# A two-layer encoder trunk on one core: order of the first norms, 20 weight subtractions behind the score's reciprocal, and one row block scaled in column halves

## The chip, the cores and the metric

The kernel runs on one core of a Trainium2 chip. The metric is the device time of one execution in microseconds (us). Before the change three runs gave 2630.57, 2634.04 and 2635.19 us; the median is 2634.04. The profile is one execution more, of 2632.38 us.

## The reference

2048 rows (frames) of 1024 numbers go through a gated MLP layer (A) and an attention layer (B), with residual adds and a last norm. All is float32.

```python
def gmlp_mixer(h, w_in, ln_g, ln_b, w_s, b_s, w_out):
    u, v, z = jnp.split(h @ w_in, 3, axis=-1)          # 1024 -> 3 x 2048
    v = layer_norm(jax.nn.gelu(v), ln_g, ln_b)
    ...
    mixed = jnp.einsum('hts,bgshc->bgthc', w_m, vg)    # within groups of 128 rows
    ...
    return (jax.nn.gelu(u) * mixed * jax.nn.silu(z)) @ w_out

def chunk_attention_mixer(h, k_pad, v_pad, w_qz, rel_bias, w_out):
    q, z = jnp.split(h @ w_qz, 2, axis=-1)
    ...
        sc = jnp.einsum('bqhd,bkhd->bhqk', qc, kc) + bias   # own chunk of 64 and 8 before
        p = jax.nn.softmax(sc, axis=-1)
        ... p @ v
    return (o * jax.nn.silu(z)) @ w_out

x = x + gmlp_mixer(rms_norm(x, a_norm_g), ...)
k, v = rms_norm(x, g_kv) @ w_kv
x = x + chunk_attention_mixer(rms_norm(x, b_norm_g), k, v, ...)
return rms_norm(x, final_norm_g)
```

## The kernel before

**Products.** A matrix product in float32 is made of three matmuls in a faster type: each operand is split into a high half (a rounded copy) and a low half (the rest), and `mm3` (lines 111 to 117) issues high x high (113) and the two mixed products (114, 115; for the projections 115 is the one with the weight's low half). A split is two instructions: ACT copies the high half, then DVE subtracts it to get the low half. For weights this is `split_in` (242 to 245): the copy is line 243, the subtraction 244. For layer A's activations and weight sums it is `split` (465 to 470, subtraction 469), for other left operands lines 362 and 367. Large products use Strassen's form with seven products, so sums of blocks are made on POOL and DVE as well.

**Start of the program (layer A, first rows).** Blocks of 128 rows are normed by `block_norm`: ACT sums the squares, DVE adds the epsilon (`power`, 744), POOL raises it to -1/2 (745), DVE scales the row (`scale`, 749). `ha0` to `ha7` are the even blocks, `hb0` on the odd ones (their `r` is `ra0` to `ra15`). PE then transposes them (643) into PSUM tiles `t0_ph_j`, and `split` makes the left operands `S0_ph_j` out of them, which frees the tile. The weight sums `T0_...`, `T1_...` are split by the same function. While `begin` is set, `first("dve", ...)` chains DVE's instructions in the order in which the code issues them.

**Attention.** Loops run over four blocks t of 512 rows, eight pairs p of heads, and eight steps u (two heads by four blocks of 128 rows). In a step `score` (1540) issues the score matmuls `s` (1555) of two steps ahead, DVE adds the bias and takes the peak in one instruction (`pr`, `nm`, 1563), ACT takes the exponential (1573), DVE the reciprocal of the sum (`sl`, 1576), POOL multiplies (1577). `flip` transposes the probabilities (`tp`, 1593), ACT copies and DVE subtracts (1597, 1598) into `pt`, and `value` multiplies by V (`pv`, 1618). Between these, PE works at the projections of the next pair: `pj{t}_{p}_{c}` with c = 1 for the queries, 0 for the keys, 2 for the gate, each of eight `mm3` on the weights `wh_b{t}_{p}_{c}` and `wl_b{t}_{p}_{c}` that `weights` (256) loads and splits, and at the output product `bo` of the block of rows before. The queries come out by ACT and DVE (`Qh`, `Ql`, 1484 and 1485), the keys by 1499 and 1500.

**Last rows.** When both halves of a block of 128 rows are done, `finish` (1908) makes its norm factor (`rr_f`), loads the row again from `x2d` and queues `scale` (1934; the DVE instruction is line 1937) in `finals`, one of which is taken in each step u and in `last_all`. Output goes through SP. In block t = 3 and pair p = 7 the rows `y2_0` to `y2_3` of block 2 are finished beside the last scores `s3_15_...`, and then `last_all` makes the output product of block 3.

**Who sets the order.** A scheduler places the instructions of all engines by its own estimates of their times; each engine then runs its list in order. Manual dependencies (`behind`, `follow`, `on_beat`, `paced`) only constrain that order, without a semaphore. SP issues most of the DMAs.

## Time and profile before

| | |
|---|---|
| time, median of three runs | 2634.04 us |
| profiled execution: time, span | 2632.38 us, 2630.6 us |
| mean granted TensorE clock | 0.998 |
| moved by DMA | 727.65 MB, 277 GB/s in the mean |
| 128 x 512 matmuls of line 113 in layer A's first products | 1248, 397 ns each as the profile counts them |
| peak (1563), exponential (1573), multiply (1577) of the scores | 256 each, 736, 764 and 814 ns in the mean |
| subtraction for attention's weights (244) | 96, 1256 ns in the mean |

Matmuls overlap in a pipeline, so a duration of 397 ns does not mean one each 397 ns: in the timeline they start some 0.23 us apart. Idle time of an engine is shown in square brackets, with what ended it.

### The profile page before, as it was taken

What the parts mean: (1) busy time and instruction counts of PE and PEld (TensorE: products, weight loads), DVE (VectorE), ACT (ScalarE), POOL (GpSimd) and SP (SyncE); (2) the same over time, 40 slices, a digit from 0 to 9 for tenths busy, and PEclk for the clock granted to TensorE, in tenths of its full rate; (3) what the DMA queues carried; (4) which work ended last, traced back from release to release, by engine and by line L of the source; (5) the groups of instructions that cost most, each with busy time, mean ns of one, the idle gap of its engine ahead of it and who ended that gap; (6) DMA issues with size and microseconds to landing.
All of it is one profiled execution on the core that took longest, in us unless ns stands there. A gap on an engine that the chain in (4) does not pass through costs nothing. (4 is left out here: it accounts for less than half of the span.)

```text
span 2630.6 us, 38030 instructions
## 1 busy us (share of the span) xinstructions
PE 2605.7 (99%) x12976; PEld 2180.0 (83%) x12976; DVE 1865.7 (71%) x2932; ACT 1311.1 (50%) x2327; POOL 891.9 (34%) x871
## 2 busy tenths in 40 slices
PE   9999999999999999999999999999999999999998
PEld 7888888888888888888888878888888888888886
DVE  6655676766667667757776767777777777876777
ACT  5422243443433434343466466666666655666554
POOL 4611335243152332302334334344333232332235
PEclk9999999999999999999999999999999999999999
DMA  7899998989988968967977587778787667875678
GB/s 290 316 345 331 344 377 311 326 317 340 329 300 306 333 225 309 344 201 261 335 267 250 170 286 234 233 240 265 251 264 264 224 207 221 289 231 185 210 231 302
DMA packets 277169, 727.65 MB, mean 277 GB/s; under 512 B 29168, under 2 KB 69104, under 8 KB 276976
## 3 DMA queue, kind: packets, MB, share of 16 engines
q1 hardware_dynamic: 268816, 707.13, 78.2%
q10 hardware_dynamic: 8160, 18.09, 1.9%
q8 instruction: 104, 1.70, 0.3%
q14 instruction: 89, 0.73, 0.1%
HBM read 535.84 MB, written 178.78 MB: 272 GB/s over the span
## 5 line engine op out<-in xcount | busy, mean ns | idle before, releaser
L113 PE MATMUL P<-T,S 128*128 128x512 f32 x1248 | 495.5, 397 | 0.0
L115 PE MATMUL P<-T,S 128*128 128x512 f32 x1248 | 488.3, 391 | 0.1
L114 PE MATMUL P<-T,S 128*128 128x512 f32 x1248 | 487.7, 391 | 0.0
L1577 POOL TENSOR_SCALAR pr<-pr,sl 128x640 f32<-128x640 f32 (+4 forms) x256 | 208.4, 814 | 551.5 <-DVE sl L1576 472.6
L113 PE MATMUL pj<-hh_b,wh_b 128*128 128x512 f32 x768 | 318.1, 414 | 0.0
L115 PE MATMUL pj<-hh_b,wl_b 128*128 128x512 f32 x768 | 304.4, 396 | 0.3 <-DVE wl_b L244 0.2
L114 PE MATMUL pj<-hl_b,wh_b 128*128 128x512 f32 x768 | 302.7, 394 | 0.0
L1573 ACT ACTIVATE pr<-pr,nm 128x640 f32<-128x640 f32 (+4 forms) x256 | 195.5, 764 | 193.8 <-DVE nm L1563 191.8
L115 PEld LDWEIGHTS P<-T,S 128*128 128x128 f32 x1248 | 234.5, 188 | 50.9 <-DVE S L469 0.4
L114 PEld LDWEIGHTS P<-T,S 128*128 128x128 f32 x1248 | 235.3, 189 | 45.1 <-DVE T L469 0.3
L113 PEld LDWEIGHTS P<-T,S 128*128 128x128 f32 x1248 | 235.1, 188 | 44.6 <-DVE vst L670 0.2
L1598 DVE TENSOR_TENSOR pt<-tp,pt 128x640 fp32r<-128x640 f32 (+4 forms) x256 | 188.8, 737 | 47.2 <-ACT pt L1597 44.2
L1563 DVE CUSTOM_DVE_ANT_0 pr<-s,bias 128x640 f32<-128x640 f32 (+4 forms) x256 | 188.3, 736 | 45.0 <-PE s L1555 38.1
L1597 ACT CAST pt<-tp 128x640 fp32r<-128x640 f32 (+4 forms) x256 | 159.0, 621 | 41.4 <-PE tp L1593 35.8
L115 PEld LDWEIGHTS pj<-hh_b,wl_b 128*128 128x128 f32 x768 | 144.2, 188 | 34.5 <-DVE wl_b L244 2.7
L1593 PE MATMUL tp<-ident,pr 128*128 128x128 f32 x1120 | 166.5, 274 | 4.7 <-DVE pt L1598 4.4
L1593 PEld LDWEIGHTS tp<-ident,pr 128*128 128x128 f32 x1120 | 130.6, 140 | 39.0 <-issue 11.9
L1618 PEld LDWEIGHTS pv<-pt,V 128*128 128x128 f32 x896 | 144.2, 190 | 19.5 <-DVE pt L1598 3.6
L113 PEld LDWEIGHTS pj<-hh_b,wh_b 128*128 128x128 f32 x768 | 145.0, 189 | 17.8 <-ACT wh_b L243 1.2
L114 PEld LDWEIGHTS pj<-hl_b,wh_b 128*128 128x128 f32 x768 | 145.0, 189 | 16.8
L1618 PE MATMUL pv<-pt,V 128*128 128x256 f32 (+3 forms) x896 | 155.8, 321 | 0.6 <-DVE pt L1598 0.5
L244 DVE TENSOR_TENSOR wl_b<-raw_b,wh_b 128x1024 fp32r<-128x1024 f32 x96 | 120.5, 1256 | 25.1 <-ACT wh_b L243 24.1
(309 smaller groups left out, 5711.7 us busy)
## 6 DMA issues: line engine op xcount, KB each, us to landing
S<-hsd SPq DMA_DIRECT2D x288, 512.0 KB, 5.5
rw<-in_w_a SPq DMA_DIRECT2D x108, 512.0 KB, 6.4
raw_b<-wk SPq DMA_DIRECT2D x75, 512.0 KB, 4.4
A<-ytd SPq DMA_DIRECT2D x72, 512.0 KB, 5.7
hsd<-S SPq DMA_DIRECT2D x56, 512.0 KB, 4.6
V<-vhd SPq DMA_DIRECT2D x56, 512.0 KB, 5.3
bias<-reld SPq DMA_DIRECT2D x64, 320.0 KB, 3.9
va<-vd SPq DMA_DIRECT2D x32, 512.0 KB, 5.5
```

The lines of the kernel that those rows point to most:

```text
L113: first = mm(ps, lh, rh, start=first, stop=False)
L114: mm(ps, lh, rl, start=False, stop=False)
L115: ends[0] = mm(ps, ll, rh, start=False, stop=last).ins.name
L244: tv(wl[:], raw[:], wh[:].bitcast(F32), op=sub)
L1563: peak = nc.vector.tensor_tensor_reduce(out=pr[:, c0:].rearrange("p (a b) -> p a b", a=nseg), in0=ps[:, :nseg, :w], in1=bias[:, c0:].rearr ...
L1573: nc.scalar.activation(pr[:, c0:], pr[:, c0:], AF.Exp, scale=-1.0, bias=nm[:], accum_out=sl[:])
L1577: nc.gpsimd.tensor_scalar(pr[:, c0:], pr[:, c0:], sl[:], 1.0, op0=ALU.mult, op1=ALU.mult)
L1593: ins = tpose(tp[:, b, :], pr[:, b * P : (b + 1) * P], ident[:])
L1597: nc.scalar.copy(oh, tp[:, b0:5, :].rearrange("p a b -> p (a b)"))
L1598: nc.vector.tensor_tensor(pt[:, 2560 + o + b0 * P : 2560 + o + 640], tp[:, b0:5, :].rearrange("p a b -> p (a b)"), oh.bitcast(F32), op=ALU ...
L1618: mm(po[:, q0 * P : q1 * P], vtl[t, p][:, i, hs], rhs, start=(i == blocks[0] and j == 0), stop=(i == 7 and j == 1),)
```

## The change

It has three parts, and no matmul is added or removed.

1. **Norming order.** `power` and `scale` are held in DVE's first order only for blocks below 8. The scale of an even block is issued one step later, and for blocks 10 and 12 (`ha5`, `ha6`) it goes behind the last scale. The weight subtractions of `T0_2` go behind the last scale, those of `T1_2` behind the last low half of a left operand. ACT's copy for `S0_1_4` goes behind the last square.
2. **Ties.** For the 20 weights in `BEHIND` the subtraction goes behind the reciprocal of the last score issued before it in the code (`recips`).
3. **Rows by halves.** The row `y2_3` is loaded as two halves; the scales of `y2_1` and `y2_3` are issued one column half at a time through `beside`: behind the peak of a score, in step u = 6 of the last pair, in `last_all`, or before the last value product.

```diff
--- before.py
+++ after.py
@@ -197,2 +197,3 @@
     beat = []
+    recips = []
 
@@ -241,7 +242,8 @@
 
-    def split_in(raw, wh, wl):
+    def split_in(raw, wh, wl, names=()):
         hi = nc.scalar.copy(wh[:], raw[:])
-        tv(wl[:], raw[:], wh[:].bitcast(F32), op=sub)
+        follow(tv(wl[:], raw[:], wh[:].bitcast(F32), op=sub), names)
         return hi
 
+    BEHIND = {1: ((2, 1), (3, 0), (4, 0), (5, 0), (7, 1), (7, 2)), 2: ((1, 0), (2, 2), (3, 2), (5, 1), (7, 1), (7, 0), (7, 2)), 3: ((1, 1), (1, 0), (4, 1), (4, 2), (5, 1), (7, 0), (7, 2))}
     kept = []
@@ -269,3 +271,3 @@
                 keep_all()
-        hi = split_in(raw, *w)
+        hi = split_in(raw, *w, recips if t and (p, c) in BEHIND[t] else ())
         if t:
@@ -464,3 +466,3 @@
 
-        def split(hi, lo, src, key=None):
+        def split(hi, lo, src, key=None, tie=None):
             ins = first("act", nc.scalar.copy(hi, src))
@@ -468,3 +470,6 @@
                 in_order(key, ins)
-            first("dve", nc.vector.tensor_tensor(lo, src, hi.bitcast(F32), op=sub))
+            low = first("dve", nc.vector.tensor_tensor(lo, src, hi.bitcast(F32), op=sub))
+            if tie:
+                behind(low, tie)
+            last["dve"] = low.ins.name
             return ins
@@ -530,3 +535,6 @@
                 out[q] = where(q)
-                ins = split(*out[q], vs[q])
+                tie = None
+                if n in (0, 1) and ph == 2:
+                    tie = last["low"] if n else last["scale"]
+                ins = split(*out[q], vs[q], tie=tie)
                 if n in (0, 1) and ph in (6, 4, 5, 7):
@@ -645,3 +653,6 @@
             t = s_tile(f"S0_{ph}_{j}")
-            split(t[:, 0], t[:, 1], pt[:], "S")
+            ins = split(t[:, 0], t[:, 1], pt[:], "S")
+            last["low"] = last["dve"]
+            if (ph, j) == (1, 4):
+                behind(ins, last["square"])
             later(1, lambda: paced(nc.sync.dma_start(
@@ -743,3 +754,5 @@
             def power():
-                first("dve", nc.vector.tensor_scalar(r[:], r[:], EPS, None, op0=add))
+                ins = nc.vector.tensor_scalar(r[:], r[:], EPS, None, op0=add)
+                if blk < 8:
+                    first("dve", ins)
                 ins = nc.gpsimd.tensor_tensor(r[:], r[:], mhalf[:], op=ALU.pow)
@@ -748,5 +761,10 @@
             def scale(c=slice(0, D)):
-                first("dve", nc.vector.scalar_tensor_tensor(
+                ins = nc.vector.scalar_tensor_tensor(
                     t[:, c], t[:, c], r[:], gab[:, c], op0=mul, op1=mul
-                ))
+                )
+                if blk < 8:
+                    first("dve", ins)
+                elif blk in (10, 12):
+                    behind(ins, last["scale"])
+                last["scale"] = ins.ins.name
 
@@ -971,3 +989,3 @@
             ts.setdefault(s, []).append(lambda: todo.pop(0)())
-            at(s + 1, lambda: todo.pop(0)())
+            at(s + 1 + (block is block_a and s >= 0), lambda: todo.pop(0)())
 
@@ -1572,2 +1590,4 @@
                 gating.pop(0)()
+            if beside:
+                beside.pop(0)(peaks[-1:])
             nc.scalar.activation(
@@ -1575,3 +1595,3 @@
             )
-            nc.vector.reciprocal(sl[:], sl[:])
+            recips[:] = [nc.vector.reciprocal(sl[:], sl[:]).ins.name]
             nc.gpsimd.tensor_scalar(
@@ -1625,2 +1645,3 @@
         gating = []
+        beside = []
         peaks = []
@@ -1846,2 +1867,4 @@
                             finals.pop(0)()
+                        while beside:
+                            beside.pop(0)()
                     if k == 1:
@@ -1922,5 +1945,6 @@
                     y = [row[b][:, c, :] for c in range(2)]
-                elif t + 2 == NT and b == 0:
+                elif t + 2 == NT and b in (0, 3):
                     on_beat(first)
-                    y = [half_tile("og", f"y{t}_{b}_{c}", 2)[:] for c in range(2)]
+                    tag, n = ("C", 4) if b else ("og", 2)
+                    y = [half_tile(tag, f"y{t}_{b}_{c}", n)[:] for c in range(2)]
                     for c in range(2):
@@ -1933,4 +1957,4 @@
 
-                def scale():
-                    for c in range(2):
+                def scale(cols=(0, 1), names=()):
+                    for c in cols:
                         cs = slice(c * 512, c * 512 + 512)
@@ -1939,2 +1963,3 @@
                         )
+                        follow(ins, names)
                         if not last:
@@ -1968,3 +1993,10 @@
                 else:
-                    finals[:0] = [scale] if t + 2 == NT else [lambda: None, scale]
+                    if t + 2 < NT:
+                        finals[:0] = [lambda: None, scale]
+                    elif closed:
+                        finals[:0] = [scale]
+                    else:
+                        finals[:0] = [lambda: beside.extend(
+                            lambda names=(), c=c: scale((c,), names) for c in range(2)
+                        )]
 
@@ -2126,2 +2158,4 @@
                         finals.pop(0)()
+                    if beside and (t + 1, p + 1, u) == (NT, NPAIR, 6):
+                        beside.pop(0)()
                     if todo:
@@ -2134,2 +2168,4 @@
                 before = t, p
+        while beside:
+            beside.pop(0)()
         value(*before, 1)
```

The first place is DVE at the start of the program. Before:

```order
L469 TENSOR_TENSOR T0_2_01_778<-rw0_2_100_545,T0_2_00_777 128x1024
L469 TENSOR_TENSOR T1_2_hl_851<-rw1_2_100_549,T1_2_hl_851 128x1024
L469 TENSOR_TENSOR T0_2_11_848<-rw0_2_101_547,T0_2_10_847 128x1024
L469 TENSOR_TENSOR T1_2_hl_851<-rw1_2_101_551,T1_2_hl_851 128x1024
L469 TENSOR_TENSOR S0_1_5_666<-t0_1_5_661,S0_1_5_666 128x512
L744 TENSOR_SCALAR ra5_558<-ra5_558 128x1
L749 SCALAR_TENSOR_TENSOR hb2_557<-hb2_557,ra5_558,gab_345 128x1024
L469 TENSOR_TENSOR S0_4_1_678<-t0_4_1_673,S0_4_1_678 128x512
L469 TENSOR_TENSOR S0_1_6_723<-t0_1_6_718,S0_1_6_723 128x512
L469 TENSOR_TENSOR S0_5_0_733<-t0_5_0_728,S0_5_0_733 128x512
```

After, from the scale of `hb2` on:

```order
L762 SCALAR_TENSOR_TENSOR hb2_557<-hb2_557,ra5_558,gab_345 128x1024
L471 TENSOR_TENSOR S0_1_5_665<-t0_1_5_660,S0_1_5_665 128x512
L471 TENSOR_TENSOR T0_2_01_778<-rw0_2_100_545,T0_2_00_777 128x1024
L471 TENSOR_TENSOR S0_4_1_677<-t0_4_1_672,S0_4_1_677 128x512
L471 TENSOR_TENSOR T0_2_11_848<-rw0_2_101_547,T0_2_10_847 128x1024
L471 TENSOR_TENSOR S0_1_6_722<-t0_1_6_717,S0_1_6_722 128x512
L471 TENSOR_TENSOR S0_5_0_733<-t0_5_0_728,S0_5_0_733 128x512
L471 TENSOR_TENSOR S0_1_7_774<-t0_1_7_769,S0_1_7_774 128x512
L471 TENSOR_TENSOR S0_5_1_789<-t0_5_1_784,S0_5_1_789 128x512
L471 TENSOR_TENSOR S0_4_2_798<-t0_4_2_793,S0_4_2_798 128x512
L471 TENSOR_TENSOR S0_2_0_844<-t0_2_0_839,S0_2_0_844 128x512
L471 TENSOR_TENSOR T1_2_hl_851<-rw1_2_100_549,T1_2_hl_851 128x1024
```

`S0_4_1` had the four weight subtractions ahead of it and now has one; the two of `T1_2_hl` stand behind `S0_2_0` and `S0_2_1`.

The second place is one tie, `wl_b3_1_0`, on DVE. Before, from that subtraction on (the reciprocal of `s3_1_0` stands two rows below the last one here):

```order
L244 TENSOR_TENSOR wl_b3_1_0_22635<-raw_b3_1_0_22633,wh_b3_1_0_22634 128x1024
L1576 RECIPROCAL sl3_0_2_22509<-sl3_0_2_22509 128x1
L367 TENSOR_TENSOR Slo2_1_1_22857<-A2_00_22514,Sho2_1_1_22856 128x512
L1640 TENSOR_TENSOR og32_2_7_22364<-pv2_15_22535,ot2_15_22561 64x512
L1598 TENSOR_TENSOR pt3_0_22552<-tp3_0_0_22553,pt3_0_22552 128x640
L1563 ISA pr3_0_3_22575,nm3_0_3_22576<-s3_0_3_22570,bias3_0_22259 128x640
L1563 ISA nm3_0_3_22576 128x1
L1648 SCALAR_TENSOR_TENSOR og2_7_22579<-og32_2_7_22364,Z2_7_22226 128x512
L1576 RECIPROCAL sl3_0_3_22577<-sl3_0_3_22577 128x1
L1598 TENSOR_TENSOR pt3_0_22552<-tp3_0_1_22592,pt3_0_22552 128x640
L1563 ISA pr3_1_0_22611,nm3_1_0_22612<-s3_1_0_22606,bias3_1_22463 128x640
L1563 ISA nm3_1_0_22612 128x1
```

After:

```order
L1581 ISA pr3_1_0_22611,nm3_1_0_22612<-s3_1_0_22606,bias3_1_22463 128x640
L1581 ISA nm3_1_0_22612 128x1
L1503 SCALAR_TENSOR_TENSOR Ql3_1_0_22622<-pj3_1_1_22531,Qh3_1_0_22621 64x512
L1961 SCALAR_TENSOR_TENSOR y1_0_22497<-y1_0_22497,rr_f1_0_22493,gf_13671 128x512
L1596 RECIPROCAL sl3_1_0_22613<-sl3_1_0_22613 128x1
L245 TENSOR_TENSOR wl_b3_1_0_22635<-raw_b3_1_0_22633,wh_b3_1_0_22634 128x1024
L1503 SCALAR_TENSOR_TENSOR Ql3_1_1_22628<-pj3_1_1_22531,Qh3_1_1_22627 64x512
L1618 TENSOR_TENSOR pt3_0_22552<-tp3_0_2_22643,pt3_0_22552 128x640
L1961 SCALAR_TENSOR_TENSOR y1_0_22497<-y1_0_22497,rr_f1_0_22493,gf_13671 128x512
```

The subtraction went from behind `Slo2_1_0` to behind the reciprocal `sl3_1_0`, and `Ql3_1_0` and the first half of `y1_0` stand ahead of that reciprocal. PE at the same place, before, from the score `s3_1_0` on:

```order
L1555 MATMUL s3_1_0_22606<-K3_0_1_22411,Qh3_0_1_22304 128x320 x2
L1555 MATMUL s3_1_0_22606<-K3_0_1_22411,Ql3_0_1_22305 128x320 x2
L113 MATMUL pj3_1_1_22531<-hh_b_13392,wh_b3_1_1_22526 128x512
L114 MATMUL pj3_1_1_22531<-hl_b_13393,wh_b3_1_1_22526 128x512
L115 MATMUL pj3_1_1_22531<-hh_b_13392,wl_b3_1_1_22527 128x512
L113 MATMUL pj3_1_0_22639<-hh_b_13392,wh_b3_1_0_22634 128x512
L114 MATMUL pj3_1_0_22639<-hl_b_13393,wh_b3_1_0_22634 128x512
L115 MATMUL pj3_1_0_22639<-hh_b_13392,wl_b3_1_0_22635 128x512
L1593 MATMUL tp3_0_2_22643<-ident_178,pr3_0_2_22507 128x128 x5
```

After, from the same score on:

```order
L1573 MATMUL s3_1_0_22606<-K3_0_1_22411,Qh3_0_1_22304 128x320 x2
L1573 MATMUL s3_1_0_22606<-K3_0_1_22411,Ql3_0_1_22305 128x320 x2
L113 MATMUL pj3_1_1_22531<-hh_b_13392,wh_b3_1_1_22526 128x512
L114 MATMUL pj3_1_1_22531<-hl_b_13393,wh_b3_1_1_22526 128x512
L115 MATMUL pj3_1_1_22531<-hh_b_13392,wl_b3_1_1_22527 128x512
L113 MATMUL pj3_1_0_22639<-hh_b_13392,wh_b3_1_0_22634 128x512
L114 MATMUL pj3_1_0_22639<-hl_b_13393,wh_b3_1_0_22634 128x512
L1613 MATMUL tp3_0_2_22643<-ident_178,pr3_0_2_22507 128x128 x5
L1573 MATMUL s3_1_1_22665<-K3_0_1_22411,Qh3_0_1_22304 128x320 x2
L1573 MATMUL s3_1_1_22665<-K3_0_1_22411,Ql3_0_1_22305 128x320 x2
L115 MATMUL pj3_1_0_22639<-hh_b_13392,wl_b3_1_0_22635 128x512
```

The first matmul on `wl_b3_1_0` now follows the transposes `tp3_0_2` and the score `s3_1_1`.

The third place is DVE beside the last scores. Before:

```order
L367 TENSOR_TENSOR Qlo_1_0_25326<-A_hh_25188,Qho_1_0_25325 128x512
L1576 RECIPROCAL sl3_15_0_25308<-sl3_15_0_25308 128x1
L1598 TENSOR_TENSOR pt3_14_25227<-tp3_14_2_25332,pt3_14_25227 128x640
L1937 SCALAR_TENSOR_TENSOR y2_1_25286<-y2_1_25286,rr_f2_1_25282,gf_13671 128x512 x2
L2005 TENSOR_TENSOR ou2_1_0_22882<-bo2_3_0_25290,ou2_1_0_22882 128x512
L1563 ISA pr3_15_1_25356,nm3_15_1_25357<-s3_15_1_25351,bias3_15_25137 128x640
L1563 ISA nm3_15_1_25357 128x1
L1598 TENSOR_TENSOR pt3_14_25227<-tp3_14_3_25366,pt3_14_25227 128x640
L1919 TENSOR_TENSOR rr_f2_3_25379<-ssq2_3_25128 128x1
L2005 TENSOR_TENSOR ou2_1_1_23227<-bo2_3_1_25347,ou2_1_1_23227 128x512
L1576 RECIPROCAL sl3_15_1_25358<-sl3_15_1_25358 128x1
```

After, from the split of `tp3_14_2` on:

```order
L1618 TENSOR_TENSOR pt3_14_25227<-tp3_14_2_25332,pt3_14_25227 128x640
L2037 TENSOR_TENSOR ou2_1_0_22882<-bo2_3_0_25290,ou2_1_0_22882 128x512
L1581 ISA pr3_15_1_25354,nm3_15_1_25355<-s3_15_1_25349,bias3_15_25137 128x640
L1581 ISA nm3_15_1_25355 128x1
L1961 SCALAR_TENSOR_TENSOR y2_1_25286<-y2_1_25286,rr_f2_1_25282,gf_13671 128x512
L1618 TENSOR_TENSOR pt3_14_25227<-tp3_14_3_25365,pt3_14_25227 128x640
L1942 TENSOR_TENSOR rr_f2_3_25377<-ssq2_3_25128 128x1
L1596 RECIPROCAL sl3_15_1_25356<-sl3_15_1_25356 128x1
L2037 TENSOR_TENSOR ou2_1_1_23227<-bo2_3_1_25345,ou2_1_1_23227 128x512
L127 TENSOR_SCALAR rr_f2_3_25377<-rr_f2_3_25377 128x1
L1581 ISA pr3_15_2_25398,nm3_15_2_25399<-s3_15_2_25393,bias3_15_25137 128x640
L1581 ISA nm3_15_2_25399 128x1
```

The two halves of `y2_1` stood together ahead of `ou2_1_0` and the peak of `s3_15_1`; now the first stands behind that peak, and the second behind that of `s3_15_2`.

## The prediction

> **What bounds the kernel now.** I read the page first, then the granted clock by stretches, then the waits of TensorE (PE), and then the timelines around the longest of them.
>
> ```profile
> PE 2605.7 (99%) x12976; PEld 2180.0 (83%) x12976; DVE 1865.7 (71%) x2932; ACT 1311.1 (50%) x2327; POOL 891.9 (34%) x871
> ...
> PE tp L1593 <- DVE pt L1598: 4.4, 10, 0.8
> PE t L643 <- DVE S L469: 2.0, 1, 2.0
> PE s L1555 <- DVE nm L1563: 1.8, 1, 1.8
> ...
> PE pj L115 <- DVE wl_b L244: 0.2, 1, 0.2
> ```
>
> PE is busy for 99% of the span, and none of its matmuls is removed or added by the change. So only its waits can move the end. Each row of the second part names who waits, who ended the wait, and total, count and longest in us. Two single waits stand out, 2.0 us near the start and 1.8 us near the end; transposes of attention (`tp`) wait 4.4 us in ten places. For the low halves of attention's weights (`wl_b`) PE waits only 0.2 us: they are early today, and the change makes 20 of them late.
>
> ```profile
> 527.56 0.63 PE L879 MATMUL ty<-ident,y 128*128 128x128 f32 x4 [1.44 <-ACT th L897]
> ...
> 527.60:531.60 4.00, 4.00 (x22) 1.00 0.64 162
> 50.20:54.00 3.80, 3.80 (x12) 0.55 1.01 363
> 2575.70:2580.50 4.80, 4.80 (x21) 0.64 0.97 222
> ```
>
> The last three rows give, for a stretch, its length, PE's busy time, then the granted clock. A wait costs more than its length if it is long: behind the waits of 2.0 and 1.8 us the clock is 0.55 and 0.64 for about 4 us, behind one of 1.44 us it is 1.00. The two losses are 3.80 x (1 - 0.55) = 1.71 us and 4.80 x (1 - 0.64) = 1.73 us. The Trainium skill ("TensorE: Matmul & The Clock Gate", section "What's actually happening") has the clock fall after an idle window of about 3.4 us. By that rule neither wait here would have cost any clock; the rows differ, so I go by a limit between 1.44 and 1.82 us.
>
> **Part one, norming order.**
>
> ```profile
> 25.81 0.66 PE L643 MATMUL t<-ident,ha 128*128 128x128 f32 x4 [1.08 <-DVE ha L749]
> ...
> 28.57 0.63 PE L643 MATMUL t<-ident,hb 128*128 128x128 f32 x4 [0.96 <-DVE ra L744]
> ...
> 49.08 1.16 PE L643 MATMUL t<-ident,hb 128*128 128x128 f32 x8 [2.05 <-DVE S L469]
> 50.00 0.48 PE L113 MATMUL P<-T,S 128*128 128x512 f32 x1
> ...
> 36.65 2.31 DVE L749 SCALAR_TENSOR_TENSOR ha<-ha,ra,gab 128x1024 f32<-128x1024 f32 x1 [2.39 <-POOL ra L745]
> 38.88 0.68 DVE L469 TENSOR_TENSOR S<-t,S 128x512 fp32r<-128x512 f32 x1
> 39.48 1.72 DVE L469 TENSOR_TENSOR T<-rw,T 128x1024 fp32r<-128x1024 f32 x1
> 41.13 2.31 DVE L469 TENSOR_TENSOR T_hl<-rw,T_hl 128x1024 fp32r<-128x1024 f32 x1
> ...
> 47.05 1.28 DVE L749 SCALAR_TENSOR_TENSOR hb<-hb,ra,gab 128x1024 f32<-128x1024 f32 x1 [0.67 <-POOL ra L745]
> 48.25 1.88 DVE L469 TENSOR_TENSOR S<-t,S 128x512 fp32r<-128x512 f32 x3
> ...
> 40.20 2.16 POOL L773 TENSOR_TENSOR ha<-hb,ha 128x512 f32<-128x512 f32 x1
> ```
>
> PE waits at 47 us for S0_4_1, the first of the three splits at 48.25, because four weight splits stand ahead of it on DVE. The new order leaves one ahead of S0_4_1, one more ahead of S0_1_6, and puts two far behind; ha5 and ha6 also go behind hb0 and hb1, which frees the 1.08 us (1.25 from matmul to matmul) and about 0.3 of the 0.96; PE is then 1.5 us ahead. But hb2 needs a power that POOL makes in an order that is not changed, behind the row at 40.20, which ended at 42.36. That work hangs on hb0, which is 1.5 us earlier, and I take 1.2 off; with 0.55 for the power hb2 begins at 41.7. Then 1.28 + 0.68 + 1.72 + 0.68 us follow (hb2, S0_1_5, T0_2_01, S0_4_1), with overlapping ends: S0_4_1 is ready at about 46.1, not 48.9. PE wants it at about 45.3, and then waits again for S0_1_6 (T0_2_11 stands ahead), until 48.3. The matmul that began at 50.00 begins at about 48.85: **-1.15 us**. What is won at 25 us is inside this figure, as the later wait swallows it. If two shorter waits keep the clock up, 1.71 us more is won (-2.86); if POOL is later by a microsecond, only about 0.3.
>
> **Part two, 20 ties.** The tie that I work in full is `wl_b3_1_0`, whose new place on DVE and PE is shown with the change:
>
> ```profile
> 2315.98 0.82 DVE L1563 CUSTOM_DVE_ANT_0 pr<-s,bias 128x640 f32<-128x640 f32 x1 [0.29 <-PE s L1555]
> 2316.73 1.22 DVE L244 TENSOR_TENSOR wl_b<-raw_b,wh_b 128x1024 fp32r<-128x1024 f32 x1
> 2317.87 0.16 DVE L1576 RECIPROCAL sl<-sl 128x1 f32<-128x1 f32 x1
> 2317.99 0.75 DVE L1937 SCALAR_TENSOR_TENSOR y<-y,rr_f,gf 128x512 f32<-128x512 f32 x1
> 2318.66 0.68 DVE L1485 SCALAR_TENSOR_TENSOR Ql<-pj,Qh 64x512 fp32r<-64x512 f32 x1
> ...
> 2316.85 0.83 ACT L1573 ACTIVATE pr<-pr,nm 128x640 f32<-128x640 f32 x1 [1.06 <-DVE nm L1563]
> 2317.68 0.58 ACT L1484 ACTIVATE Qh<-pj 64x512 fp32r<-64x512 f32 x1
> ...
> 2315.40 0.45 PE L1555 MATMUL s<-K,Ql 128*128 128x320 f32 x2
> 2316.15 0.40 PE L115 MATMUL pj<-hh_b,wl_b 128*128 128x512 f32 x1
> ```
>
> A score's chain runs from PE's last score matmul (ends 2315.85) over peak (0.82), exponential (0.83) and reciprocal (0.16); a tied subtraction adds 1.22. With the four hand-overs (0.4 together in these rows) that is 3.42 us at the least. PE's new order gives it less here: behind the score, from 2315.69, stand five matmuls of 0.23 us, a group of transposes (0.55) and the next score (0.6), so the first matmul on the low half is wanted at 2317.99. And the chain isn't at its least. On ACT Qh now stands ahead of the exponential; it waits for the projection that ends at 2316.55, so the exponential ends at 2318.0. On DVE Ql and a row scale y1_0 (0.68 + 0.75) come first, then the reciprocal at 2318.7, and the low half is ready at 2320.0: PE waits **2.0 us** (1.85 of them idle, as the profile counts it). Everything behind that subtraction on DVE (Ql of the second head, the next transposes' split, the next peak) is later too, but PE waits anyway.
>
> The same done for the other 19, with each one's rows: weights (t,p,c) (1,2,1), (1,3,0), (1,4,0) 0.5 each; (1,5,0) 0; (1,7,1) 1.0; (1,7,2) 0.1; (2,1,0) 1.65; (2,2,2), (2,3,2) 0.45 each; (2,5,1) 0.55; (2,7,1) 0.3; (2,7,0) 0.8; (2,7,2) 0.85; (3,1,1) 1.0; (3,4,1) 0.45; (3,4,2) 0; (3,5,1) 0.85; (3,7,0) 0.2; (3,7,2) 0.3. Sum with the first: 12.4 us. If every chain took only 3.42 us, the sum would be 4.9: that is the floor. DVE's order is fixed and other rows do stand in most chains, so I stay near the upper figure, at 11.
>
> What comes back: subtractions no longer stand ahead of splits that PE waits for.
>
> ```profile
> 1992.98 0.41 PE L1593 MATMUL tp<-ident,pr 128*128 128x128 f32 x2 [0.39 <-DVE pt L1598]
> 1999.94 0.50 PE L115 MATMUL pj<-hh_b,wl_b 128*128 128x512 f32 x1 [0.24 <-DVE wl_b L244]
> 2023.60 0.74 PE L1593 MATMUL tp<-ident,pr 128*128 128x128 f32 x5 [0.42 <-DVE pt L1598]
> 2262.45 0.41 PE L1593 MATMUL tp<-ident,pr 128*128 128x128 f32 x2 [0.79 <-DVE pt L1598]
> ```
>
> At all four a tied (or, at 1999.94, a neighbouring) subtraction moves out of the way: 0.39 + 0.24 + 0.42 + 0.79 = 1.84 us, and 0.16 each that PE needs to start again, 2.5 us. I add 1.0 for shorter waits right behind a tie, which a later PE no longer meets (an estimate, out of the 4.4 us). Net of part two: 11 - 3.5 = **+7.5 us**; with the floor 4.9 - 3.5 = +1.4.
>
> ```profile
> 1804.46 1.21 DVE L244 TENSOR_TENSOR wl_b<-raw_b,wh_b 128x1024 fp32r<-128x1024 f32 x1
> 1790.91 1.68 DVE L244 TENSOR_TENSOR wl_b<-raw_b,wh_b 128x1024 fp32r<-128x1024 f32 x1
> ...
> 1804.72 1.62 POOL L1577 TENSOR_SCALAR pr<-pr,sl 128x640 f32<-128x640 f32 x1 [1.38 <-DVE sl L1576]
> 1790.72 0.80 POOL L1577 TENSOR_SCALAR pr<-pr,sl 128x640 f32<-128x640 f32 x1
> ```
>
> A tie sets the subtraction beside POOL's multiply, which the same reciprocal releases. Where POOL began first (1790.72) the subtraction took 1.68 us; where it began first itself, right behind a reciprocal (1804.46), it kept 1.21 and POOL took 1.62. A tie has the second order, so I add nothing; POOL's 0.8 us are covered by the several us between a score and its transposes. The Trainium skill ("GPSIMD Engine Reference", section "1. Specifications") says that POOL contends with DVE instructions of two SBUF inputs, and this subtraction is one; if it were the subtraction that paid each time, 20 x 0.47 = 9.4 us would be added to the chains. The row at 1804.46 speaks against that.
>
> **Part three, rows by halves.**
>
> ```profile
> 2571.31 2.98 DVE L1937 SCALAR_TENSOR_TENSOR y<-y,rr_f,gf 128x512 f32<-128x512 f32 x2 [0.42 <-POOL rr_f L128]
> 2574.82 0.81 DVE L1563 CUSTOM_DVE_ANT_0 pr<-s,bias 128x640 f32<-128x640 f32 x1
> 2575.69 0.56 PE L1555 MATMUL s<-K,Qh 128*128 128x320 f32 x2 [1.82 <-DVE nm L1563]
> ```
>
> The two halves of y2_1 stand ahead of the peak whose end frees the score buffer. Behind the change one stands behind that peak and one behind the next. DVE is free at 2570.9 (the split ahead), the sum `ou2_1_0` takes 0.68 and the peak 0.81: it ends at 2572.4, and PE wants the buffer at 2572.3. So 1.99 us (the wait and its 0.16) and the 1.73 us of clock go. Late next is the split of the transposed weights pt3_14, for which the first half row (0.75 us alone, 1.8 beside POOL) stands ahead: 2575.0 at worst, where `pv` wants it at 2574.3. I charge 0.9 for both: **-2.85 us**. In the best case -3.6, in the worst -1.0 (the split 1.8 us later, and the clock falls). The row loads that SP now issues later (row2, y2_0) have readers well behind them in the timeline, and SP itself no longer waits there for both halves of y2_3, so I charge nothing for them.
>
> **Sum.** -1.15 + 7.5 - 2.85 = +3.5 us. Against the profiled execution (span 2630.6 us, time 2632.38) that is 2635.9. The median of the runs, 2634.04, is 1.7 above that execution, so I write **2636 us**, near no change. 0.2% is 5.3 us, about what a measurement of this kernel can tell from no change.
>
> **Rivals.**
> - Slower (chance 0.36): the ties' chains come in full, and the wait for `wl_b3_1_0` costs clock. It decides from a wait of between 1.44 and 1.82 us, and I have 1.85 there; the price is a further 1.73 us as at 2575.70. 12.4 - 2.5 + 1.73 - 1.15 - 2.85 = +7.6: 2640 us from the profiled execution, 2641.7 from the median. For it speaks that DVE's order is fixed; against it that rows behind the moved subtractions start up to 1.2 us earlier. By the skill's gate rule above the 1.73 would not come.
> - Faster (0.13): chains at their floor and the clock kept at the start: +1.4 - 2.86 - 3.6 = -5.1, so 2627. Against it: the rows that stand between score and reciprocal in at least seven ties.
> - The halves don't do what they say (0.1, within no change): the wait goes from the score to `pv`. -1.0 in place of -2.85: 2637.7.
>
> The forecast itself has 0.41. No change then has 0.51, slower 0.36, faster 0.13. The range takes in the faster rival's upper part and the slower one, with a spread of 2 us between runs: 2629 to 2643.
>
> **What would show it.** In the waits of PE the row `pj <- wl_b` should grow from 0.2 to about 9 to 12 us in some 15 places, the longest at the weight (3,1,0); were it under 5, the chains are at their floor or below. The row `s <- nm` of 1.8 should go, and with it the clock of 0.64 near 2576. The wait of 2.05 at 49 us should break into two of about 1.1. I am wrong if the subtractions end before PE wants them, or if the waits they take away on `tp` were more than 3.5 us of the 4.4.

## The result and the profile after

| | before | after |
|---|---|---|
| median of the runs, us | 2632.84 (6 runs, 2629.99 to 2635.19) | 2641.34 (6 runs, 2639.94 to 2642.32) |
| ratio | | 1.0033 (95% interval 1.0023 to 1.0043) |
| profiled execution, us | 2632.38 | 2641.83 |
| its span, us | 2630.6 | 2640.0 |
| from PE's last matmul to the end, us | 7.33 | 8.98 |

The change makes the kernel 0.33% slower, by 8.5 us of the medians. The interval of the ratio leaves out 1, and 8.5 us are more than the 5.3 that the prediction took for about what a measurement of this kernel can tell from no change. The likeliest case, no change at 2636, didn't come; the time is 5.3 us above it, within the range, and at the slower rival's 2640 to 2641.7.

The page's line of busy times and PE's waits in the changed kernel (who waits, who ended the wait; total, count and longest in us):

```profile
PE 2607.2 (99%) x12976; PEld 2178.6 (83%) x12976; DVE 1870.5 (71%) x2932; ACT 1310.6 (50%) x2327; POOL 905.1 (34%) x871
...
PE tp L1613 <- DVE pt L1618: 6.5, 12, 1.7
PE pj L115 <- DVE wl_b L245: 6.4, 13, 1.7
PE t L651 <- DVE S L471: 2.0, 2, 1.5
...
PE bo L115 <- DVE Slo L369: 0.9, 1, 0.9
...
PE pv L1638 <- DVE pt L1618: 0.8, 3, 0.4
```

The wait for `wl_b` grew from 0.2 to 6.4 us, which is what the ties had to show. Three things were not in the forecast: the transposes' row grew too (4.4 to 6.5, longest 1.7), a row for `Slo` came up, and `pv` waits in three places for 0.8 us in place of 0.5 in one. The row `s <- nm` of 1.8 is gone.

To see where the time lies, I set both traces side by side by the work that PE has done: how much later, in us, the changed kernel reaches the same work.

| before's time, us | 30 | 50 | 60 | 1700 | 1980 | 2040 | 2060 | 2300 | 2320 | 2560 | 2580 | 2600 | PE's end | span's end |
|---|---|---|---|---|---|---|---|---|---|---|---|---|---|---|
| after, later by | -1.5 | -1.7 | -3.3 | -2.6 | +0.4 | -0.1 | +2.1 | +5.2 | +8.1 | +9.7 | +6.4 | +8.3 | +7.7 | +9.4 |

The start wins 3.3 us, the long stretch up to 1700 loses 0.7, the section with the ties (1700 to 2560) loses 12.3, the stretch from there to PE's end wins 1.9, and the tail behind PE's last matmul loses 1.65.

**The tie worked in full.** DVE, ACT and PE of the changed kernel around `wl_b3_1_0`, in order of time (start, us, engine, line, operation; in brackets the idle time ahead and who ended it):

```profile
2322.18 0.82 DVE L1581 CUSTOM_DVE_ANT_0 pr<-s,bias 128x640 f32<-128x640 f32 x1 [0.52 <-PE s L1573]
...
2323.41 0.68 DVE L1503 SCALAR_TENSOR_TENSOR Ql<-pj,Qh 64x512 fp32r<-64x512 f32 x1 [0.39 <-ACT Qh L1502]
2324.01 0.73 DVE L1961 SCALAR_TENSOR_TENSOR y<-y,rr_f,gf 128x512 f32<-128x512 f32 x1
2324.67 0.15 DVE L1596 RECIPROCAL sl<-sl 128x1 f32<-128x1 f32 x1
2324.75 1.20 DVE L245 TENSOR_TENSOR wl_b<-raw_b,wh_b 128x1024 fp32r<-128x1024 f32 x1
...
2322.78 0.59 ACT L1502 ACTIVATE Qh<-pj 64x512 fp32r<-64x512 f32 x1 [1.98 <-PE pj L115]
2323.28 0.82 ACT L1593 ACTIVATE pr<-pr,nm 128x640 f32<-128x640 f32 x1
...
2326.00 0.50 PE L115 MATMUL pj<-hh_b,wl_b 128*128 128x512 f32 x1 [1.67 <-DVE wl_b L245]
```

This is the chain of the prediction, row by row: peak, Qh ahead of the exponential, Ql and the row scale ahead of the reciprocal, and only then the subtraction, which ends at 2325.95. PE starts again at 2326.00; the wait is 1.67 us idle, where 1.85 were predicted. The granted clock was 1.00 over the 4 us behind it.

**A wait that wasn't foreseen.** The issue of the next raw out weight on SP's queue, before:

```profile
2026.28 0.45 SPq L290 DMA_DIRECT2D raw_bo<-in_wb_out  x1
```

After: the subtraction of the tied low half on DVE, the last store of queries and the same issue, with the one after it in one row, on SP's queue, what ACT does then, and PE's next transposes:

```profile
2027.39 1.20 DVE L245 TENSOR_TENSOR wl_b<-raw_b,wh_b 128x1024 fp32r<-128x1024 f32 x1
...
2029.35 0.49 SPq L1508 DMA_DIRECT2D Ql<-Ql  x1
2029.89 2.59 SPq L292 DMA_DIRECT2D raw_bo<-in_wb_out  x2
...
2037.23 1.05 ACT L244 CAST wh_bo<-raw_bo 128x1024 fp32r<-128x1024 f32 x1 [4.07 <-DMA raw_bo<-in_wb_out]
2038.18 0.83 ACT L1593 ACTIVATE pr<-pr,nm 128x640 f32<-128x640 f32 x1
...
2041.57 0.69 ACT L1617 CAST pt<-tp 128x640 fp32r<-128x640 f32 x1
...
2043.92 0.30 PE L1613 MATMUL tp<-ident,pr 128*128 128x128 f32 x1 [1.68 <-DVE pt L1618]
```

Attention's weights and the out weights share two raw buffers (`wr`). The low half of weight (2,1,0) is subtracted at 2027.39 in the changed kernel, behind a reciprocal, and holds its raw buffer until 2028.59. The order on SP's queue is another one too: the four stores of `Qh` and `Ql`, which stood behind this load before (2028.85 to 2031.03), now stand ahead of it. So the load of the next raw out weight is issued at 2029.89, right behind the last of them and 3.6 us later than before; how much of this is the buffer and how much SP's order wasn't separated. ACT's next row is the cast of that weight: it stands idle for 4.07 us (2.59 before), and an exponential and the copy of the transposes stand behind it. So in this execution a tie that costs 1.38 us at its own place costs 1.86 us (1.68 idle) again 15 us later. In three other kernels with this tie the second loss is 0.6 to 1.1 us; a table below has the rows.

**The last pair.** PE's waits of the changed kernel from 2574 to 2602:

```profile
2581.09 0.74 PE L1613 MATMUL tp<-ident,pr 128*128 128x128 f32 x5 [0.98 <-DVE pt L1618]
2590.41 0.74 PE L1613 MATMUL tp<-ident,pr 128*128 128x128 f32 x5 [0.56 <-DVE pt L1618]
2593.60 0.74 PE L1613 MATMUL tp<-ident,pr 128*128 128x128 f32 x5 [0.40 <-DVE pt L1618]
2596.64 0.74 PE L1613 MATMUL tp<-ident,pr 128*128 128x128 f32 x5 [0.20 <-DVE pt L1618]
```

The score no longer waits, and the clock doesn't fall (1.00 over 2584 to 2590); but four groups of transposes wait for the split of the group before, 2.14 us in all.

**The tail.** ACT's order near the end, before:

```
L1893 ACTIVATE jk_110_25767,ssq_1_25766<-row_25629 128x512
L362 CAST Qho_0_25803<-A_hl 128x512
L1893 ACTIVATE jk_111_25791,ssq_3_25790<-row_25631 128x512
L362 CAST Qho_1_25826<-A_hl 128x512
```

After:

```
L1916 ACTIVATE jk_110_25769,ssq_1_25768<-row_25629 128x512
L1916 ACTIVATE jk_111_25793,ssq_3_25792<-row_25631 128x512
L364 CAST Qho_0_25805<-A_hl 128x512
L364 CAST Qho_1_25828<-A_hl 128x512
```

and DVE there in the changed kernel:

```profile
2622.41 0.69 DVE L2015 TENSOR_TENSOR row<-bo,row 128x512 f32<-128x512 f32 x1 [1.18 <-POOL row L2033]
...
2624.41 2.85 DVE L369 TENSOR_TENSOR Qlo<-A_hl,Qho 128x512 fp32r<-128x512 f32 x2 [0.70 <-ACT Qho L364]
2627.18 1.27 DVE L2037 TENSOR_TENSOR row<-bo,ou 128x512 f32<-128x512 f32 x2
```

The square sum `jk_111` stands ahead of both casts, so that both splits begin late; DVE, which also waits 1.18 us for a sum of POOL, runs behind PE, and the last row sums with it. The ties stand 60 us and more ahead of this place: the order of the program's end was changed with them all the same.

### The profile page after: what moved, and what is told of

The parts are those of the page before. It is cut to its first block, busy times and chain, and to the rows that moved or that the text cites. A ratio compares the mean times of both kernels' runs of the same rounds, so it can differ in the third digit from the quotient of the medians.

```text
span 2640.0 us, 37989 instructions
## 1 busy us (share of the span) xinstructions
PE 2607.2 (99%) x12976; PEld 2178.6 (83%) x12976; DVE 1870.5 (71%) x2932; ACT 1310.6 (50%) x2327; POOL 905.1 (34%) x871
## 5 line engine op out<-in xcount | busy, mean ns | idle before, releaser
L1597 POOL TENSOR_SCALAR pr<-pr,sl 128x640 f32<-128x640 f32 (+4 forms) x256 | 226.1, 884 | 542.4 <-DVE sl L1596 468.7
```

Source lines behind the costliest of these rows:

```text
L1597: nc.gpsimd.tensor_scalar(pr[:, c0:], pr[:, c0:], sl[:], 1.0, op0=ALU.mult, op1=ALU.mult)
```

## The experiments

Each ratio below is to the kernel before, run beside it. Three theories stood at first for the loss of 9.4 us. The one I took up: the ties cost about 12 us, since what they delay waits at places that I had not charged. Its rivals: the ties cost the 7.5 us of the prediction and another part costs the rest, or the clock does.

**Part one alone** (norming order; nothing of the ties and the halves). Its edit is the diff's lines in `split`, `finish`, `power`, `scale` and the delayed call:

```diff
-                ins = split(*out[q], vs[q])
+                if n in (0, 1) and ph == 2:
+                    tie = last["low"] if n else last["scale"]
+                ins = split(*out[q], vs[q], tie=tie)
...
+                if blk < 8:
+                    first("dve", ins)
+                elif blk in (10, 12):
+                    behind(ins, last["scale"])
...
-            at(s + 1, lambda: todo.pop(0)())
+            at(s + 1 + (block is block_a and s >= 0), lambda: todo.pop(0)())
```

> The norming order alone, put into the kernel before. Theory (each part acts alone): -3.3 us against before, the PE wait of 2.05 us at 47 us broken up and no stretch below a clock of 0.9 at 50 to 54 us. Rival (the gain at the start is handed back at the first wait for a transfer or an ACT table further on): between -1 and 0 us.

Measured: 2629.69 us (11 runs), ratio 0.9990 (0.9981 to 0.9999). PE is 1.8 us earlier at 50 us and 3.4 at 60, where the clock didn't fall. That is the theory's 3.3 at its place; the interval of the whole time, 0.3 to 5 us faster, fits it and doesn't shut out the rival's 1.

**Part two alone** (the 20 ties):

```diff
-        hi = split_in(raw, *w)
+        hi = split_in(raw, *w, recips if t and (p, c) in BEHIND[t] else ())
```

> The 20 ties alone, put into the kernel before. Theory (PE waits for the tied low halves and for what stands behind them): +12 us against before, PE's wait for wl_b 6 to 7 us and the wait of tp up by about 2. Rival (the ties cost only my sum of first waits, the rest of the loss comes from the other two parts): +7.5 us.

Measured: 2646.07 us (5 runs), ratio 1.0056 (1.0044 to 1.0069): PE loses 11.6 us between 1700 and 2560, and the tail is 8.86 us. The theory's 12 us came, the 7.5 fell.

**Part three alone** (row scale by halves):

```diff
-                    finals[:0] = [scale] if t + 2 == NT else [lambda: None, scale]
+                        finals[:0] = [lambda: beside.extend(
+                            lambda names=(), c=c: scale((c,), names) for c in range(2)
+                        )]
```

> The rows by halves alone, put into the kernel before. Theory: PE's last matmul ends about 1.9 us earlier (the wait of 1.82 us and the clock of 0.64 near 2576 us go, some transposes wait 0.2 to 1 us instead), but the tail behind it is 1.6 us longer, so -0.3 us in all. Rival (the longer tail comes from the ties, which shift PE against the last transfers): -1.9 us and a tail of 7.3 us.

Measured: 2630.74 us (11 runs), ratio 0.9992 (0.9983 to 1.0000). PE wins 3.9 us by 2580 and gives back 1.65 by 2600. The tail is 7.13 us: it isn't this part that lengthens it, as I had thought.

**Parts one and three, without ties** (the changed kernel with an empty table):

```diff
+    BEHIND = {1: (), 2: (), 3: ()}
```

> The change without the ties (the table of ties empty). Theory: the sum of the first and third parts, -3.6 us against before, about 2629 us. Rival (the parts act on each other, PE being earlier meets later weights or transfers): no better than -1 us.

Measured: 2628.27 us (11 runs), ratio 0.9982 (0.9973 to 0.9992), faster than both kernels, as the theory's sum had it. PE's waits in it over the section of the ties, 1696 to 2556, in two rows:

```profile
PE tp L1613 <- DVE pt L1618: 3.0, 6, 0.8
PE pj L115 <- DVE wl_b L245: 0.4, 2, 0.2
```

The changed kernel has all of its rows for `wl_b`, `Slo` and `pv` in this section (1697 to 2569 there), and for the transposes:

```profile
PE tp L1613 <- DVE pt L1618: 3.5, 5, 1.7
```

The transposes wait no less with the ties than without: the 1.7 that is new takes the place of the shorter waits that go.

**The kernel before, once more,** unchanged, for the clock:

> The kernel before, unchanged, profiled once more. Theory (whether TensorE's clock falls after a wait of about 2 us is a matter of chance): the waits of 2.0 us near 47 us and 1.8 us near 2574 are there again, but at least one of the two stretches behind them has a clock above 0.9. Rival (the clock falls after every wait of over 1.7 us): both stretches at 0.55 to 0.65 again.

Measured: 2631.11 us (one run). PE's two long waits:

```profile
49.22 1.16 PE L643 MATMUL t<-ident,hb 128*128 128x128 f32 x8 [2.05 <-DVE S L469]
...
2574.09 0.56 PE L1555 MATMUL s<-K,Qh 128*128 128x320 f32 x2 [1.86 <-DVE nm L1563]
```

The stretches behind them (length, busy times of the engines, granted clock, then DMA share and GB/s):

```profile
51.00:55.00 4.00, 4.00 (x20) 3.30 (x19) 1.15 (x2) 0.59 (x1) 1.48 (x2) 1.00 1.03 338
...
2574.00:2578.00 4.00, 3.91 (x14) 3.52 (x15) 3.69 (x12) 2.46 (x7) 1.88 (x3) 0.57 0.92 229
```

The wait of 2.05 us that cost clock in the first profile (0.55) cost none here, and the shorter one cost it both times. So a limit in us, as I had drawn it, doesn't decide alone.

**One tie alone,** (2,1,0), with parts one and three, for the wait at 2041:

```diff
+    BEHIND = {1: (), 2: ((1, 0),), 3: ()}
```

> The change with one tie only, that of weight (2,1,0). Theory: PE loses 2.2 to 2.7 us between 2020 and 2060 us against the same kernel without ties: a wait of 1.2 us for the tied low half and one of 1.7 us of the transposes of the second head, less 0.4 that goes. Rival (the second wait comes from the ties before this one): about 0.9 us, and no wait of over 0.5 us of the transposes there.

Measured: 2630.87 us (one run); against the kernel without ties PE loses 2.2 us from 2020 to 2060.

```profile
2028.05 0.50 PE L115 MATMUL pj<-hh_b,wl_b 128*128 128x512 f32 x1 [1.23 <-DVE wl_b L245]
2042.11 0.74 PE L1613 MATMUL tp<-ident,pr 128*128 128x128 f32 x5 [0.46 <-DVE pt L1618]
...
2035.42 1.05 ACT L244 CAST wh_bo<-raw_bo 128x1024 fp32r<-128x1024 f32 x1 [2.84 <-DMA raw_bo<-in_wb_out]
```

The loss is at the theory's lower end, but the second wait is 0.46 us idle, not 1.7. Here are the four kernels in which this tie stands behind the reciprocal and the cast isn't moved; that with the ties of t = 2 follows below:

| kernel | load issued behind PE's first matmul on the tied half, us | issue to landing, us | ACT idle ahead of the cast, us | transposes idle, us |
|---|---|---|---|---|
| one tie | 1.2 | 6.1 | 2.84 | 0.46 |
| the ties of t = 2 | 1.2 | 6.2 | 2.94 | 0.56 |
| part two alone | 1.2 | 6.6 | 3.33 | 0.94 |
| the changed kernel | 1.2 | 7.3 | 4.07 | 1.68 |

The load is issued at the same point each time. What differs is how long it takes to land, and both idle times grow by as much. So about 0.5 us of the 1.68 comes with the tie, and 1.2 with a load that took longer in this execution. Why it did is open: each kernel has one profile.

**The same with the cast moved:** the cast of that raw out weight is put behind the last exponential issued, so that it can't stop the exponentials.

```diff
+                    elif (t, ph) == (1, 1):
+                        follow(hi, exps)
```

> The same one tie, and in addition ACT's copy of the output weight wh_bo1_1_0 goes behind the exponential that was issued last before it. Theory (the tied subtraction holds one of two raw weight buffers, the next load into it lands late, and the copy that waits for that load stops ACT, which runs in order): the wait of 1.7 us of the transposes goes, that of 1.2 us for the low half stays, 0.7 to 1.2 us lost in all. Rival (the transposes wait because the tied subtraction itself delays DVE): the wait of 1.7 us stays.

Measured: 2634.29 us (one run; it loses 3 us before 1540, ahead of the place). PE's waits from 2030 on:

```profile
2030.71 0.50 PE L115 MATMUL pj<-hh_b,wl_b 128*128 128x512 f32 x1 [1.23 <-DVE wl_b L246]
2049.73 0.56 PE L1576 MATMUL s<-K,Qh 128*128 128x320 f32 x2 [1.03 <-DVE nm L1584]
2051.25 0.50 PE L114 MATMUL bo<-wl_bo,Sho 128*128 128x512 f32 x1 [0.21 <-DVE wl_bo L246]
```

The transposes' wait at 2042 is gone, which shows that it came through ACT's stop at the load. But the row that was moved is waited for later, and a score waits 1.03 us in its place: from 2020 to 2070 PE loses 3.1 us against the kernel without ties, with one tie alone 2.2. The 0.7 to 1.2 us that the theory named didn't come.

**The ties behind the peak** in place of the reciprocal, for all 20, which takes the exponential and the reciprocal out of each chain:

```diff
-        hi = split_in(raw, *w, recips if t and (p, c) in BEHIND[t] else ())
+        hi = split_in(raw, *w, peaks[-1:] if t and (p, c) in BEHIND[t] else ())
```

> The change with the same 20 weights tied behind the last score's peak, one step earlier in its chain than the reciprocal. Theory (a tie costs what its chain is longer than PE's work up to the first use): without the exponential, the reciprocal and two hand-overs the chain is 1.2 us shorter, so that of the 13 waits for low halves two or three are left, together under 1.5 us, and the time is 2628 to 2633 us. Rival (any subtraction placed between the steps of a score costs, by what it pushes back on DVE and ACT): waits for transposes take their place, and the time stays above 2636 us.

Measured: 2637.36 us (11 runs), ratio 1.0018 (1.0009 to 1.0027). PE's waits over 1697 to 2565:

```profile
PE tp L1613 <- DVE pt L1618: 2.4, 5, 0.8
PE pj L115 <- DVE wl_b L245: 2.4, 6, 0.7
PE pv L1638 <- DVE pt L1618: 1.4, 5, 0.4
PE pv L1638 <- ACT pt L1617: 1.0, 1, 1.0
```

The waits for `wl_b` fall from 6.4 to 2.4, as a shorter chain should have it, but `pv` waits more, and the time stays over the theory's 2628 to 2633. PE's loss in the section against the kernel before is 7.9 us, not 12.3. So both had a part: the shorter chain takes a third off the loss, and `pv` waits more, which fits the rival's view that a subtraction between two steps pushes back what stands behind it. The time is the rival's; the waits are those of `pv`, and not of the transposes as it named them.

**The ties of one layer of row blocks at a time** (t = 1, 2, 3), with parts one and three; the table of each, in this order:

```diff
+    BEHIND = {1: ((2, 1), (3, 0), (4, 0), (5, 0), (7, 1), (7, 2)), 2: (), 3: ()}
...
+    BEHIND = {1: (), 2: ((1, 0), (2, 2), (3, 2), (5, 1), (7, 1), (7, 0), (7, 2)), 3: ()}
...
+    BEHIND = {1: (), 2: (), 3: ((1, 1), (1, 0), (4, 1), (4, 2), (5, 1), (7, 0), (7, 2))}
```

> Parts 1 and 3, with the six ties of weights (1,p,c) alone. Theory (the loss is made at each tie, where TensorE waits, and isn't made up later): TensorE loses against the kernel without ties what it loses in the changed kernel up to 1980 us, 4.9 us in all, and the tail behind the last matmul stays at 7.3 us as without ties; 2628.3 + 4.9 = 2633. Rival (the losses overlap: a TensorE that is late at one tie no longer meets the next wait): this layer alone loses under 3.5 us of it by the end of the section, since later waits are swallowed; 2630 to 2631.5.

> Parts 1 and 3, with the seven ties of weights (2,p,c) alone. Theory: +4.9 us between 2000 and 2290 us, as in the changed kernel there, of it some 2.2 at 2020 to 2060 (the wait at the tied low half and that of the transposes behind it); tail 7.3 us; 2633. Rival: the transposes' wait at 2041 needs the ties of layer 1 ahead of it, so that it is under 0.7 us here, as with the one tie; then +3.7 and 2632.

> Parts 1 and 3, with the seven ties of weights (3,p,c) alone. Theory: +4.3 us from 2300 to 2560 us, of it 1.8 at weight (3,1,0); and here alone of the three the tail behind the last matmul is 8.9 us in place of 7.3, since these ties change ScalarE's order at the very end (the square sum of the last but one row stands ahead of the two casts for the last products), while TensorE gets 0.6 back before it: 2628.3 + 4.3 + 1.6 - 0.6 = 2633.6. Rival: the tail hangs on how late TensorE and the row loads are at the end and not on that order; then all three layers have a tail of 7.3 to 7.9 and this one is at 2632.

| ties | median, us | ratio (95%) | PE's loss 1700 to 2560 against no ties, us | tail, us |
|---|---|---|---|---|
| none | 2628.27 | 0.9982 (0.9973 to 0.9992) | | 7.28 |
| t = 1 | 2630.78 | 0.9993 (0.9983 to 1.0002) | 2.2 | 7.26 |
| t = 2 | 2633.23 | 1.0005 (0.9995 to 1.0014) | 5.0 | 6.82 |
| t = 3 | 2633.26 | 1.0004 (0.9994 to 1.0013) | 4.1 | 9.02 |
| all | 2641.34 | 1.0033 (1.0023 to 1.0043) | 12.8 | 8.98 |

The losses come from one profile of each kernel; over the same stretch the two profiles of the kernel before differ by 0.2 us. The three losses add up to 11.3 of the 12.8. Had later waits swallowed what an earlier layer costs, they would add up to more than the whole: nothing of that shows, and 1.5 us come only with all three, of it 1.1 with the slow load at 2041. With t = 1 the time is the rival's, but not for its reason: PE loses 2.6 us from 1700 to 2000 there, and 2.7 in the changed kernel. My 4.9 held 1.1 us that the changed kernel had lost before 1700, and left out the 1.1 it wins back at 2000. With t = 2 the sum came as the theory had it, and the single wait stayed under the rival's 0.7:

```profile
2024.97 0.50 PE L115 MATMUL pj<-hh_b,wl_b 128*128 128x512 f32 x1 [1.23 <-DVE wl_b L245]
2039.14 0.74 PE L1613 MATMUL tp<-ident,pr 128*128 128x128 f32 x5 [0.56 <-DVE pt L1618]
```

But the ties of t = 1 ahead of it, which the rival held necessary, don't decide it: part two alone has them, and waits 0.94. As the table above shows, it goes by the landing of the load. With t = 3, and with none of the other two, the tail is the long one, and PE wins 0.8 us from 2600 to 2620 ahead of it. ACT has the changed kernel's order at the end in this kernel alone of the three. The order is not the whole of it: the kernel with the ties behind the peak has that order too, with a tail of 7.65 us; its PE waits 0.79 us ahead of the tail, and its DVE doesn't wait for POOL's sum. What else decides it is open.

**The tie of (3,1,0) alone:**

```diff
+    BEHIND = {1: (), 2: (), 3: ((1, 0),)}
```

> Parts 1 and 3, with the single tie of weight (3,1,0), which the prediction worked in full at 2.0 us of wait. Theory: TensorE waits 1.7 to 2.0 us for this low half near 2310 us as in the changed kernel (1.83), loses as much there against the kernel without ties, and nothing else: span 2624.5 + 1.8 = 2626.3, 1 us either way by chance. Rival: without the tie of (3,1,1) ahead of it and its wait at pv (0.64 in the changed kernel) the wait is longer, 2.4 us, and the net is the same 1.8.

Measured: 2630.34 us (one run). PE waits 1.67 us idle at 2316.74, as in the changed kernel, and loses 1.9 us between 2300 and 2320. The rival's longer wait of 2.4 didn't come. The span of 2628.6 is 4.1 over that of the kernel without ties, not 1.8: the two differ by 1.8 already at 1700, ahead of any tie. So single profiles of two such kernels can't settle a difference of 2 us in the whole time.

## Why the prediction was right and where it failed

All terms are against the profiled execution of before, in us.

| step | predicted | measured |
|---|---|---|
| part one, waits | -1.15 | -1.7 |
| part one, clock (only in its best case) | 0 | -1.6 |
| part two, waits at the tied halves | +11 | +9.8 |
| part two, waits that go | -3.5 | -3.2 |
| part two, new waits elsewhere | 0 | +4.8 |
| part two, smaller waits and gaps (the rest of the section's 12.3) | 0 | +0.9 |
| part two, tail | 0 | +1.65 |
| part three | -2.85 | -1.9 |
| before 1700, in rows that no part touches | 0 | +0.7 |
| sum | +3.5 | +9.4 |

The measured time lies within the range, 5.3 us above the value written. It does so by the width of the range, and because errors of both signs met: 7.35 us came from terms that stood at nothing, and 2.15 were won back at the start beyond what was forecast.

**Part two is the step that failed,** and in one term above all: the new waits elsewhere, which stood at nothing and measured 4.8 us. The waits at the tied halves, counted from matmul to matmul over the usual 0.23 us, came in 15 places, and one more of 0.24, and add up to 9.8 of the 11 that I took: (3,1,0) 1.83 (predicted 2.0), (2,1,0) 1.38 (1.65), (1,7,1) 1.05 (1.0), (1,2,1), (1,3,0), (1,4,0) about 0.5 each (0.5 each). Not every place came as worked out: (2,7,0) 0.24 (0.8), (2,7,2) 0.35 (0.85), (3,1,1) 0.31 (1.0) and (3,5,1) 0.37 (0.85) were short, (2,7,1) and (3,4,1) with 0.59 each (0.3 and 0.45) longer. What I took from below, the floor of 4.9, was far off, and staying near the upper figure was right. The waits that go (0.55 at 1992, 0.41 at 1999, 0.59 at 2023, 0.47 of 0.96 at 2261, 0.49 at 1774 and smaller ones) give the 3.2 of the 3.5.

What I set to nothing is what the moved subtraction holds up besides PE: its raw buffer, with the load that waits for it, and DVE. I wrote of (3,1,0) that everything behind it on DVE is later too, "but PE waits anyway". It doesn't wait anyway at the next place: transposes at 2041.84 +1.86, `Slo` at 1971.90 +1.03, `pv` at 2311.60 +0.64, three more of 0.4 to 0.5, 4.8 in all. The one at 2041 comes through ACT, which stands at a cast whose load was issued 3.6 us later; moving the cast took that wait away. Its size is in part luck: the load also took 7.3 us to land, where other kernels with the tie had 6.1 to 6.6. For the one at 1971.90 the runs show that it comes with the ties of t = 1 (0.8 us with these alone, no such row without ties). The traces point to the same way there: in the three kernels that have these ties behind the reciprocal, a raw out weight is loaded at 1963 to 1964 us, in the others at 1930 to 1936, and ACT stands idle for 1.9 to 2.1 us at its cast just ahead of the place, in the others not at all. No run tried it by itself, and none had a third raw buffer.

**The tail** was not in the sum at all. The order was to be had ahead of time, and I read it at the ties and not at the program's end; there a square sum had moved ahead of two casts. It goes with the ties of t = 3: the three kernels that have all of them behind the reciprocal (changed, part two alone, t = 3 alone) have tails of 8.9 to 9.0 us, the other eleven profiles 6.8 to 7.9, the one with the ties behind the peak (7.65) among them.

**Part one** had its order of waits right and its size somewhat low. The 2.05 us broke into two, as foreseen, of 0.54 and 1.50 us in the changed kernel; together they are as long as the one they replace. So the 1.65 us won at 25 us were not swallowed, which I had reckoned, but kept. The clock kept, too: over 50.20 to 54.00 it is 1.00, and 0.55 before.

```profile
50.20:54.00 3.80, 3.80 (x19) 3.13 (x18) 0.69 (x1) 0.59 (x1) 0.00 (x0) 1.00 0.97 303
```

**Part three** did what it says; PE wins 1.9 of 2.85 from 2560 to its end, 0.6 of it only behind 2600, with the order of the tail. What is late next was named rightly, the splits of the transposed weights, but they stop the following transposes, not `pv`, and they take 2.14 us in four places and not 0.9. Part one alone, which keeps the old row scale and whose clock didn't fall there, shows the same debt: it has the score's wait and two of the transposes, 3.55 us in all, where the kernel without ties has 1.78.

```profile
2566.84 0.74 PE L1609 MATMUL tp<-ident,pr 128*128 128x128 f32 x5 [0.64 <-DVE pt L1614]
2571.40 0.56 PE L1571 MATMUL s<-K,Qh 128*128 128x320 f32 x2 [1.75 <-DVE nm L1579]
2581.53 0.74 PE L1609 MATMUL tp<-ident,pr 128*128 128x128 f32 x5 [1.16 <-DVE pt L1614]
```

So this part wins 1.8 us with the clock up as well. In the kernel before, a throttled PE reaches the transposes too late to meet the third of these waits.

**The rivals.** The slower one named the right time for a reason that was half wrong, so its time was luck: chains for the most part (9.8 of 12.4), but no clock lost behind (3,1,0), where it had put 1.73, and new waits and a tail that it didn't have. Its point of decision, a wait of between 1.44 and 1.82 us, isn't one. The halves' rival fell, since the wait didn't go to `pv`. The faster one fell: the waits at the ties add up to 9.8, and not to the 4.9 of its floor.

**POOL beside the subtractions** was rightly charged at nothing. The tied subtraction at 2324.75 took 1.20 us. The multiplies and the subtractions before, then after (count, busy us and mean ns, then idle time ahead):

```profile
L1577 POOL TENSOR_SCALAR pr<-pr,sl 128x640 f32<-128x640 f32 (+4 forms) x256 | 208.4, 814 | 551.5 <-DVE sl L1576 472.6
L244 DVE TENSOR_TENSOR wl_b<-raw_b,wh_b 128x1024 fp32r<-128x1024 f32 x96 | 120.5, 1256 | 25.1 <-ACT wh_b L243 24.1
...
L1597 POOL TENSOR_SCALAR pr<-pr,sl 128x640 f32<-128x640 f32 (+4 forms) x256 | 226.1, 884 | 542.4 <-DVE sl L1596 468.7
L245 DVE TENSOR_TENSOR wl_b<-raw_b,wh_b 128x1024 fp32r<-128x1024 f32 x96 | 116.8, 1222 | 23.6 <-ACT wh_b L244 21.7
```

POOL's multiplies take 17.7 us more, and DVE's subtractions 3.7 less: POOL pays. The port rule that the prediction weighed (the Trainium skill, "GPSIMD Engine Reference", "1. Specifications") says that the two contend; these numbers agree, and put the price on POOL here.

## What to carry to other kernels

Before a row is moved to a later place, follow not only who waits for its result but also what it holds meanwhile: here a raw buffer, whose next load came late and stopped the engine that reads it, with all that stood behind on that engine, cost 0.6 to 1.9 us beside the tie's own 1.4. A wait that a cover no longer hides is to be looked for one stage further on, and the order at the program's end belongs among the places to read, even when the edit is far from it. A long wait that costs clock can also hide the wait behind it, so that taking the first away gives less than its length and the clock together.
